# Binary cross-entropy on one core: the last chunk's predictions move in unequal pieces at both ends, and the side block goes

## The chip, the cores and the metric

The kernel runs on one core of one Trainium2 chip. The metric is device time in microseconds (us), the median of several runs; lower is better. Beside it stands one profiled execution, whose trace gives every instruction and every packet of the sixteen DMA engines. The engines named below are PE (TensorE, unused here), DVE (VectorE), ACT (ScalarE), POOL (GpSimd) and SP (SyncE). POOL and SP do no arithmetic here: they issue transfers, each from a queue of its own, in program order.

## The reference

```python
"pred": np.random.uniform(0.01, 0.99, (8192, 8192)).astype(np.float32),
"target": np.random.randint(0, 2, (8192, 8192)).astype(np.float32),
...
eps = 1e-7
pred = np.clip(pred, eps, 1 - eps)
return -(target * np.log(pred) + (1 - target) * np.log(1 - pred))
```

Each element stands alone, so the arrays can be cut in any way. Two arrays of 268 MB are read and one is written.

## The kernel before

A target is 0 or 1, so the loss is minus the logarithm of the absolute value of (target - 1 + pred). The kernel uses this: `front_of` (L89) clips the predictions on VectorE (L90), adds target minus 1 on VectorE (L93), takes the absolute value on ScalarE (L96) and the logarithm on ScalarE (L97). `back_of` (L99) changes the sign on VectorE (L100). All passes work in place on the predictions.

The flat arrays are taken from the end to the front in 37 chunks. Each is 128 partitions wide, with so many columns: two of 7680, then 32 of 15360, then two of 7680 and one of 1696. Spots in on-chip memory are given by `plan` (L15): two rings, one for predictions (float32) and one for targets (bfloat16, cast by the transfer on its way in), each with two places of 15360 columns used in turn, and a third small place for the last chunk alone. The last chunk is short by 352 columns, because the very first 45056 elements are a block of their own, the side block: 32 partitions of 1408, moved by SP in transfers of eight rows each, every fourth partition (L60 to L62, L78 to L87). It has two tiles of its own and goes through the same passes.

The order is written out by hand, and every engine follows it in program order. `load(k)` (L69) issues the targets of chunk k on POOL (L71) and the predictions on POOL (L72), for chunk 0 on SP. `store(k)` (L74) issues on POOL (L76), for the last three chunks on SP. In the main loop (L120) chunk k is worked in two halves and stored, and then chunk k+2 is loaded into the place that k leaves: its targets at once, its predictions after the whole store of k has landed. That wait is POOL's at L72, and what stands behind it on POOL is the next store.

The last four chunks are called z, a, b and c (L132). Chunk z has 15360 columns; a and b are the two halves, which share the place that chunk n-5 leaves; c is the small one. On VectorE the sign change of z's second half (L139) comes after both passes of chunk a (L138), and the store of z (L140) after that. Stores a, b and c are SP's. The target and prediction loads of a, b and c are all issued at the end of the last turn of the loop (L130 and L131).

A transfer runs on DMA engines in packets, one for each row of a partition: a chunk of 15360 columns is 128 packets of 61440 bytes for predictions, eight on each of the sixteen engines. Queue 0 in the trace is POOL's, queue 1 is SP's.

Of the kernel before, what the change touches and what calls it, by code (L numbers as in the profile page):

```python
# [1 line left out]

# [4 lines left out]

EPS = 1e-7

BIG = 15 * 1024  # L10
HALF = BIG // 2
SIDE = 1408


def plan(total):  # L15

    n, last = divmod(total, BIG)
    assert n > 4 and 0 < last <= 2048
    spots = [(HALF, 0), (HALF, HALF)]
    spots += [(BIG, k % 2 * BIG) for k in range(1, n - 1)]  # L20
    end = (n - 1) % 2 * BIG
    return spots + [(HALF, end), (HALF, end + HALF), (last - SIDE // 4, 2 * BIG)]

@with_exitstack
def kernel(
    ctx: ExitStack,
    tc: tile.TileContext,
    pred: bass.AP,  # L30
    target: bass.AP,
    out: bass.AP,
):
    nc = tc.nc
    fp32 = mybir.dt.float32
    bf16 = mybir.dt.bfloat16
    Alu = mybir.AluOpType
    Act = mybir.ActivationFunctionType
    P = nc.NUM_PARTITIONS

    R, C = pred.shape
    spots = plan(R * C // P)
    n = len(spots)
    widths = [w for w, _ in spots]
    cols = [sum(widths[:k]) for k in range(n)]

    def chunk(ap, k):
        flat = ap.rearrange("r c -> (r c)")
        end = R * C - cols[k] * P
        return flat[end - widths[k] * P : end].rearrange("(p w) -> p w", p=P)  # L50

    pool = ctx.enter_context(tc.tile_pool(name="rings", bufs=1))
    ring = [P, 2 * BIG + widths[-1]]
    ring_p = pool.tile(ring, fp32, name="ring_p", tag="ring_p")
    ring_t = pool.tile(ring, bf16, name="ring_t", tag="ring_t")
    warm = pool.tile([1, 8], fp32, name="warm", tag="warm")
    side_p = pool.tile([32, SIDE], fp32, name="side_p", tag="side_p")
    side_t = pool.tile([32, SIDE], fp32, name="side_t", tag="side_t")

    def side(ap, j):  # L60
        flat = ap.rearrange("r c -> (r c)")
        return flat[: 32 * SIDE].rearrange("(p w) -> p w", p=32)[j:32:4]  # L62

    def spot(ring, k, part=(0, 1)):
        w, c = spots[k]
        i, m = part
        return ring[:, c + i * w // m : c + (i + 1) * w // m]

    def load(k):  # L69
        queue = nc.sync if k == 0 else nc.gpsimd  # L70
        nc.gpsimd.dma_start(out=spot(ring_t, k), in_=chunk(target, k))  # L71
        queue.dma_start(out=spot(ring_p, k), in_=chunk(pred, k))  # L72

    def store(k):  # L74
        queue = nc.sync if k >= n - 3 else nc.gpsimd
        queue.dma_start(out=chunk(out, k), in_=spot(ring_p, k))  # L76

    def load_side():  # L78
        nc.vector.memset(side_p[:, 0:2], 0.5)  # L79
        nc.vector.memset(side_t[:, 0:2], 0.0)  # L80
        for j in range(4):
            nc.sync.dma_start(out=side_t[j:32:4, :], in_=side(target, j))
            nc.sync.dma_start(out=side_p[j:32:4, :], in_=side(pred, j))

    def store_side():
        for j in range(4):
            nc.sync.dma_start(out=side(out, j), in_=side_p[j:32:4, :])  # L87

    def front_of(p, t):  # L89
        nc.vector.tensor_scalar(  # L90
            out=p, in0=p, scalar1=EPS, scalar2=1 - EPS, op0=Alu.max, op1=Alu.min
        )
        nc.vector.scalar_tensor_tensor(  # L93
            out=p, in0=t, scalar=1.0, in1=p, op0=Alu.subtract, op1=Alu.add
        )
        nc.scalar.activation(out=p, in_=p, func=Act.Abs)  # L96
        nc.scalar.activation(out=p, in_=p, func=Act.Ln)  # L97

    def back_of(p):  # L99
        nc.vector.tensor_scalar(out=p, in0=p, scalar1=-1.0, scalar2=None, op0=Alu.mult)  # L100

    def front(k, *part):
        front_of(spot(ring_p, k, *part), spot(ring_t, k, *part))

    def back(k, *part):
        back_of(spot(ring_p, k, *part))

    with tc.manual_schedule():
        nc.vector.memset(warm, 1.0)  # L109
        for k in range(3):  # L110
            load(k)
        nc.scalar.activation(out=warm, in_=warm, func=Act.Ln)  # L112
        front(0)
        front(1)
        back(0)
        store(0)
        back(1)
        store(1)
        load(3)
        for k in range(2, n - 4):  # L120
            front(k, (0, 2))
            front(k, (1, 2))
            back(k, (0, 2))
            back(k, (1, 2))
            store(k)
            if k == n - 6:
                load_side()
            if k == n - 5:
                front_of(side_p, side_t)
            for j in range(k + 2, n if k == n - 5 else k + 3):  # L130
                load(j)  # L131
        z, a, b, c = range(n - 4, n)  # L132
        front(z, (0, 2))
        back_of(side_p)
        store_side()
        front(z, (1, 2))
        back(z, (0, 2))
        front(a)  # L138
        back(z, (1, 2))  # L139
        store(z)  # L140
        front(b, (0, 2))
        front(b, (1, 2))
        back(a)
        store(a)
        front(c)
        back(b)
        store(b)
        back(c)
        store(c)


# [1 line left out]
_INS = ['pred', 'target']  # L153
_OUTS = [((8192, 8192), 'float32')]


# [23 lines left out]
```

## Time and profile before

| What | Value | Where from |
|---|---|---|
| Time | 1864.74 us, median of 3 (1864.71, 1864.74, 1867.43) | times |
| Profiled execution: span | 1863.1 us | page |
| Profiled execution: its time | the span is all that is recorded of it; it lies 1.65 us below the median | page, times |
| Main memory read, written | 536.87 MB, 268.44 MB; 432 GB/s over the span | page, DMA queues |
| Store, issue to landing (15360 columns) | 29.2 us, median | page, DMA issues |
| Prediction load, issue to landing (15360) | 35.9 us, median | page, DMA issues |
| One transfer issue on POOL | 0.53 to 0.54 us | page, groups |
| Side block's passes | VectorE 0.87, 1.61 and 0.87 us; ScalarE 1.38 and 1.38 us | page, groups |

The page gives the busy share of each engine over the span, then the span in forty slices, then the DMA queues, the chain that ended last, and the costliest groups. The chain through the end of the kernel is read as start, length and what it was:

```profile
1749.26 4.17 DVE ring_p L100
1753.43 0.28 issue
1753.72 29.18 DMA out_dram<-ring_p
1782.89 0.28 issue
1783.18 18.44 DMA ring_p<-in_pred_dram
```

The store of chunk n-5 is issued at 1753.7 and has landed 29.18 us later; then the predictions of chunk a may be loaded into its place, and they land 18.44 us after that.

The side block's transfers stand in the list of issues with count, size and line:

```profile
side_t<-in_target_dram SPq DMA_DIRECT2D x4, 44.0 KB
side_p<-in_pred_dram SPq DMA_DIRECT2D x4, 44.0 KB
out_dram<-side_p SPq DMA_DIRECT2D x4, 44.0 KB
```

### The profile page before, as it was taken

The numbers are of one execution on the slowest core, as the hardware profiler recorded it, in microseconds if no ns is written. First come the engines' busy times: TensorE is split into PE (matmuls) and PEld (weight loads), VectorE is DVE, ScalarE is ACT, GpSimd is POOL, SyncE is SP. The second block draws the span as 40 slices with busy tenths as digits, with TensorE's granted clock in tenths as the row PEclk, the third lists the DMA queues.
The fourth block names the chain that finished last, engine by engine and source line by source line (L and its number), as shares of the span: only waits on it lengthen the run. The fifth ranks groups of instructions, "written<-read, shape, count | busy, mean of one in ns | idle before, by whom it ended". The sixth has DMA issues, their size and how long they took to land.

```text
span 1863.1 us, 649 instructions
## 1 busy us (share of the span) xinstructions
DVE 1124.7 (60%) x215; ACT 902.1 (48%) x144; POOL 57.4 (3%) x111
## 2 busy tenths in 40 slices
DVE  4655767555576655557665555766555576655585
ACT  3345553335555333555533355553335555333665
POOL 0000000000000000000000000000000000000000
DMA  9999999999999999999999999999999999999999
GB/s 295 378 356 343 352 344 367 383 385 348 348 352 344 370 384 383 347 352 351 346 370 385 383 347 352 351 346 370 385 383 346 352 352 346 370 384 379 352 340 392
DMA packets 16180, 671.22 MB, mean 360 GB/s; under 512 B 1872, under 2 KB 1872, under 8 KB 2352
## 3 DMA queue, kind: packets, MB, share of 16 engines
q0 software_dynamic: 15408, 657.98, 98.5%
q1 hardware_dynamic: 768, 13.21, 1.7%
q14 instruction: 4, 0.03, 0.0%
HBM read 536.87 MB, written 268.44 MB: 432 GB/s over the span
## 4 chain that ended last, share of the span: by engine, by line
DMA 35%; issue 26%; ACT 22%; DVE 15%; POOL 1%; DVEq 0%; POOLq 0%; PEldq 0%
DMA ring_p<-in_pred_dram 32%; ACT ring_p L96 11%; ACT ring_p L97 11%; DVE ring_p L93 7%; DVE ring_p L90 4%; DVE ring_p L100 4%; DMA out_dram<-ring_p 3%; POOL ring_t L71 0%; POOL out_dram L76 0%; DVEq L175 0%; POOL ring_p L72 0%; POOLq L76 0%; POOLq L71 0%; DVEq L90 0%; PEldq L175 0%
## 5 line engine op out<-in xcount | busy, mean ns | idle before, releaser
L96 ACT ACTIVATE ring_p<-ring_p 128x7680 f32<-128x7680 f32 (+1 forms) x70 | 450.3, 6433 | 932.2 <-DVE ring_p L93 932.2
L93 DVE SCALAR_TENSOR_TENSOR ring_p<-ring_t,ring_p 128x7680 f32<-128x7680 bf16 (+1 forms) x70 | 556.9, 7955 | 2.4
L90 DVE TENSOR_SCALAR ring_p<-ring_p 128x7680 f32<-128x7680 f32 (+1 forms) x70 | 283.8, 4055 | 396.7 <-DMA ring_p<-in_pred_dram 396.7
L100 DVE TENSOR_SCALAR ring_p<-ring_p 128x7680 f32<-128x7680 f32 (+1 forms) x69 | 283.8, 4115 | 321.2 <-ACT ring_p L97 321.2
L97 ACT ACTIVATE ring_p<-ring_p 128x7680 f32<-128x7680 f32 (+1 forms) x70 | 450.8, 6440 | 2.2
L72 POOL DMA_DIRECT2D ring_p<-in_pred_dram x36 | 19.2, 532 | 909.3 <-DMA out_dram<-ring_p 909.3
L76 POOL DMA_DIRECT2D out_dram<-ring_p x34 | 18.4, 541 | 851.3 <-DVE ring_p L100 827.0
L71 POOL DMA_DIRECT2D ring_t<-in_target_dram x37 | 20.0, 542 | 0.8 <-PEq L175 0.8
L96 ACT ACTIVATE side_p<-side_p 32x1408 f32<-32x1408 f32 x1 | 1.4, 1375 | 6.7 <-DVE side_p L93 6.7
L112 ACT ACT_TABLE_LOAD x1 | 1.3, 1283 | 0.7 <-PEq L164 0.7
L93 DVE SCALAR_TENSOR_TENSOR side_p<-side_t,side_p 32x1408 f32<-32x1408 f32 x1 | 1.6, 1611 | 0.0
L97 ACT ACTIVATE side_p<-side_p 32x1408 f32<-32x1408 f32 x1 | 1.4, 1375 | 0.0
L90 DVE TENSOR_SCALAR side_p<-side_p 32x1408 f32<-32x1408 f32 x1 | 0.9, 874 | 0.0
L100 DVE TENSOR_SCALAR side_p<-side_p 32x1408 f32<-32x1408 f32 x1 | 0.9, 874 | 0.0
L109 DVE MEMSET warm<- 1x8 f32 x1 | 0.1, 65 | 0.8 <-PEq L164 0.8
L112 ACT ACTIVATE warm<-warm 1x8 f32<-1x8 f32 x1 | 0.2, 209 | 0.0
L164 POOL MEMSET const-float32-0.0<- 128x1 f32 x1 | 0.1, 99 | 0.2 <-issue 0.2
L164 POOL MEMSET const-bfloat16-1.0<- 128x1 bf16 x1 | 0.1, 102 | 0.0
L164 POOL MEMSET const-float32-1.0<- 128x1 f32 x1 | 0.1, 99 | 0.0
L164 POOL MEMSET const-uint8-127<- 128x1 uint8 x1 | 0.1, 99 | 0.0
L79 DVE MEMSET side_p<- 32x2 f32 x1 | 0.1, 60 | 0.0
L80 DVE MEMSET side_t<- 32x2 f32 x1 | 0.1, 60 | 0.0
## 6 DMA issues: line engine op xcount, KB each, us to landing
ring_p<-in_pred_dram POOLq DMA_DIRECT2D x32, 7680.0 KB, 35.9
out_dram<-ring_p POOLq DMA_DIRECT2D x32, 7680.0 KB, 29.2
ring_t<-in_target_dram POOLq DMA_DIRECT2D x32, 3840.0 KB, 46.8
ring_p<-in_pred_dram POOLq DMA_DIRECT2D x3, 3840.0 KB, 35.6
ring_t<-in_target_dram POOLq DMA_DIRECT2D x4, 1920.0 KB, 27.9
out_dram<-ring_p POOLq DMA_DIRECT2D x2, 3840.0 KB, 27.1
out_dram<-ring_p SPq DMA_DIRECT2D x2, 3840.0 KB
ring_p<-in_pred_dram SPq DMA_DIRECT2D x1, 3840.0 KB
```

Source lines behind the costliest of these rows:

```text
L71: nc.gpsimd.dma_start(out=spot(ring_t, k), in_=chunk(target, k))
L72: queue.dma_start(out=spot(ring_p, k), in_=chunk(pred, k))
L76: queue.dma_start(out=chunk(out, k), in_=spot(ring_p, k))
L79: nc.vector.memset(side_p[:, 0:2], 0.5)
L80: nc.vector.memset(side_t[:, 0:2], 0.0)
L90: nc.vector.tensor_scalar(out=p, in0=p, scalar1=EPS, scalar2=1 - EPS, op0=Alu.max, op1=Alu.min)
L93: nc.vector.scalar_tensor_tensor(out=p, in0=t, scalar=1.0, in1=p, op0=Alu.subtract, op1=Alu.add)
L96: nc.scalar.activation(out=p, in_=p, func=Act.Abs)
L97: nc.scalar.activation(out=p, in_=p, func=Act.Ln)
L100: nc.vector.tensor_scalar(out=p, in0=p, scalar1=-1.0, scalar2=None, op0=Alu.mult)
L112: nc.scalar.activation(out=warm, in_=warm, func=Act.Ln)
L164: nc = _bacc.Bacc("TRN2", target_bir_lowering=False, num_devices=1)
```

## The change

The side block, its tiles, its transfers and its passes are gone. The last chunk has its full 2048 columns. Its rows are dealt out otherwise: the first 262144 elements are seen as (b a w) with b = 8, a = 16 and w = 2048, and partition 8a + b holds row 16b + a (`mixed`).

Its predictions come in pieces. A piece (j, lo, hi) covers the 32 partitions from 32j and the columns from 256 lo to 256 hi; in main memory its outer dimension is 4. Four pieces are issued after load 2, of widths 8, 6, 4 and 2 (in units of 256 columns) for j = 0, 1, 2, 3; three more after load 3, of widths 6, 4 and 2 for j = 3, 2, 1. Its targets are one transfer, issued where they were issued before. Its result is stored in eight pieces, on POOL instead of SP. All seven early pieces and the eight late ones are POOL's.

On POOL the early pieces stand ahead of the store of chunk 0, and ahead of the store of chunk 2. The eight late pieces stand behind the store of z, at the end of the queue. POOL's transfers take eight semaphores in turn, so the fourth early piece waits for the first target load, and the last late piece waits for the store of z.

```diff
-SIDE = 1408
+STEP = 256
+EARLY = ((0, 0, 8), (1, 0, 6), (2, 0, 4), (3, 0, 2), (3, 2, 8), (2, 4, 8), (1, 6, 8))
+LATE = (
+    (0, 0, 8), (1, 0, 1), (2, 0, 4), (3, 0, 6),
+    (1, 2, 8), (1, 1, 2), (3, 6, 8), (2, 4, 8),
+)
...
-    return spots + [(HALF, end), (HALF, end + HALF), (last - SIDE // 4, 2 * BIG)]
+    return spots + [(HALF, end), (HALF, end + HALF), (last, 2 * BIG)]
...
+    def mixed(ap):
+        flat = ap.rearrange("r c -> (r c)")[: widths[-1] * P]
+        return flat.rearrange("(b a w) -> a b w", b=8, a=16)
+
+    def tooth_of(ap, j, lo, hi):
+        return mixed(ap)[4 * j : 4 * j + 4, :, lo * STEP : hi * STEP]
+
+    def tooth_in(j, lo, hi):
+        return spot(ring_p, n - 1)[32 * j : 32 * j + 32, lo * STEP : hi * STEP]
+
+    def load_teeth(teeth):
+        for tooth in teeth:
+            nc.gpsimd.dma_start(out=tooth_in(*tooth), in_=tooth_of(pred, *tooth))
+
+    def store_teeth(teeth):
+        for tooth in teeth:
+            nc.gpsimd.dma_start(out=tooth_of(out, *tooth), in_=tooth_in(*tooth))
...
         for k in range(3):
             load(k)
+        load_teeth(EARLY[:4])
...
         load(3)
+        load_teeth(EARLY[4:])
...
-            if k == n - 6:
-                load_side()
-            if k == n - 5:
-                front_of(side_p, side_t)
-            for j in range(k + 2, n if k == n - 5 else k + 3):
+            for j in range(k + 2, n - 1 if k == n - 5 else k + 3):
                 load(j)
+        nc.gpsimd.dma_start(out=spot(ring_t, n - 1), in_=mixed(target))
         z, a, b, c = range(n - 4, n)
         front(z, (0, 2))
-        back_of(side_p)
-        store_side()
...
         back(c)
-        store(c)
+        store_teeth(LATE)
```

More of the change, by code (lines that the diff above doesn't have):

```diff
@@ L56 @@
     warm = pool.tile([1, 8], fp32, name="warm", tag="warm")
[L57 to L62, printed above, removed]
     def spot(ring, k, part=(0, 1)):
@@ L76, in store @@
         queue.dma_start(out=chunk(out, k), in_=spot(ring_p, k))
[L78 to L87, printed above, removed]
+    def mixed(ap):
[11 more added lines that the diff above has]
+            nc.gpsimd.dma_start(out=tooth_of(out, *tooth), in_=tooth_in(*tooth))
     def front_of(p, t):
```

## The prediction

> **What bounds the kernel now.** I read the busy shares first, then the table of windows, then the list of waits, then the timeline of the end, and last the records of single DMA packets.
>
> ```profile
> span 1863.1 us, 649 instructions
> DVE 1124.7 (60%) x215; ACT 902.1 (48%) x144; POOL 57.4 (3%) x111
> DMA  9999999999999999999999999999999999999999
> q0 software_dynamic: 15408, 657.98, 98.5%
> q1 hardware_dynamic: 768, 13.21, 1.7%
> ```
>
> No compute engine is busy above 60%, while the sixteen DMA engines are busy in every slice; the two queues add up to 100.2% of their time, since packets overlap a little. The windows say where that stops.
>
> ```profile
> 0.00:2.00 2.00, 0.07 (x1) 1.26 (x1) 0.96 (x6) 1.00 0.63 154
> ...
> 700.00:1700.00 1000.00, 602.48 (x113) 490.10 (x75) 29.41 (x56) 1.00 1.00 361
> ...
> 1820.00:1859.00 39.00, 24.41 (x9) 23.83 (x8) 0.00 (x0) 1.00 0.99 425
> 1859.00:1863.10 4.10, 0.00 (x0) 0.00 (x0) 0.00 (x0) 1.00 0.31 129
> ```
>
> The last-but-one column is the DMA share: 1.00 over the middle, 0.99 to 1859, then 0.31. Only the last 4 us leave engines idle. So the time is the work of the engine that ends last, plus its idle time, plus 2.0 us before the first packet and 1.05 us from the last packet (1862.05) to the end.
>
> ```profile
> POOL ring_p L72 <- DMA out_dram<-ring_p: 909.3, 32, 29.2
> DVE ring_p L90 <- DMA ring_p<-in_pred_dram: 396.7, 36, 18.5
> ```
>
> These waits are long, but the engines have queued packets under them. One stage has little cover, the end:
>
> ```profile
> 1801.71 4.16 DVE L90 TENSOR_SCALAR ring_p<-ring_p 128x7680 f32<-128x7680 f32 x1 [7.08 <-DMA ring_p<-in_pred_dram]
> 1805.91 8.16 DVE L93 SCALAR_TENSOR_TENSOR ring_p<-ring_t,ring_p 128x7680 f32<-128x7680 bf16 x1
> 1813.98 4.15 DVE L100 TENSOR_SCALAR ring_p<-ring_p 128x7680 f32<-128x7680 f32 x1
> 1818.43 0.54 POOL L76 DMA_DIRECT2D out_dram<-ring_p  x1 [32.62 <-DVE ring_p L100]
> ...
> 1836.52 9.95 SPq L76 DMA_DIRECT2D out_dram<-ring_p  x3
> ```
>
> VectorE works in order, so the store of z (L76 on POOL) waits for chunk a's predictions on all sixteen engines (1801.7), a's first two passes and z's sign change. Its first packets start at 1819.85, 1.42 us after the issue began; three engines had by then been empty for 0.2 us. Those three pay again at 1838.2, where store a arrives just as they finish z: their first packets take 1.81 to 1.98 us instead of 1.138.
>
> **Packet prices.** 61440 B take 2267 ns, 30720 B 1138, 6784 B 258: about 9 ns plus 0.03675 ns a byte. By that line, less 3 ns of overlap, eight rows cost 2.46 us at 8192 B, 1.85 at 6144, 1.25 at 4096, 0.65 at 2048 and 0.35 at 1024.
>
> **Collisions and drift.** At 73 us, where the third load ends and the first store begins, the sixteen last load packets take 2.48 to 3.23 us, together 9.6 us too much. The next such borders cost 3.0, 2.8, 0.4, 2.8, 0.9, 2.0, 1.2, 1.2, 1.2 and 1.4 us, then almost nothing. All come to 27 engine-us, 1.7 us a mean engine. Chained by start times, the engines lie 0.7 us apart at 26 us and 3.9 us apart from 856 us on (1.4 ahead of the mean to 2.5 behind). They end between 1859.2 and 1862.05, mean 1860.65.
>
> **The change part by part.**
>
> *Side block gone.* Its 96 packets of 5632 B (221 ns) fall away. The records show eight completion writes per side transfer, sixteen per whole one, so it used eight engines: 12 x 0.22 = 2.6 us on those, 1.35 us a mean engine. Its vector and scalar passes (3.4 and 2.8 us) lay in idle time: nothing.
>
> *Last chunk.* Its old load and store of predictions (8 x 0.255 = 2.04 us each) go; its target load grows from 2.03 to 2.45 us an engine (1696 to 2048 wide).
>
> *Pieces.* Early ones, if successive transfers take successive groups of four engines: group 0 gets widths 8 and 6 (2.46 + 1.85 = 4.31 us), group 1 3.10, group 2 1.90, group 3 0.65. Late ones go on with group 3: 4.31 there, then 0.70, 1.90 and 3.10 on groups 0, 1, 2. Each group has 5.0 us in all. Work per engine: minus 2.04, 2.04 and 1.35, plus 0.42, 5.0 and some 0.15 for completion writes: +0.1 us, level.
>
> [...] No transfer of before on POOL uses fewer than sixteen engines.
>
> *POOL's queue.* Fifteen issues of 0.54 us join. The fourth early piece waits for the first target load's semaphore; behind it stands the store of chunk 0, not ready before 56.6. The next three follow load 3 (95.6), ahead of a store due at 119.8. The last late piece waits for store z (landed by 1843); the late issues begin about 1846.3 and end about 1850.6, under stores a and b (running to 1857). SP loses thirteen issues; its two stores wait on VectorE as before. Cover holds: nothing. Without it each POOL issue would add its 0.54 us.
>
> *Collisions with groups apart.* Gain between 0 and 1.7 us a mean engine. With four engines together instead of sixteen I take half: 0.9 remains. A latest engine may keep between 0 and 4.2 (1.7 + 2.5).
>
> *The gate at the end.* The stagger must be paid where all engines wait for the slowest. Old loads b, target c and predictions c kept an engine busy for 22.2 us after a's predictions; without the last load it is 18.1 + 2.45 = 20.55. Store z arrives 18.15 us after the slowest landing. So an engine more than 2.4 us ahead runs dry. Group 3 is 3.66 us ahead of group 0: it idles 1.3 us or more and ends last.
>
> *Sum along group 3.* The three early engines of before go from 1819.85 to 1857.13 (z, a, b and both stalls); group 3 repeats that, then 4.31 of late pieces, 1.05 of closing: 1862.5, shifted by d, by which a's predictions land later. Before, the mean engine ended the last load at 1822.0 and the latest at 1823.7. Without side and collisions the mean is 1822.0 - 1.35 - 1.7 = 1818.95; group 0 has 4.31 more and 0.35 of initial spread: 1823.6, so d = -0.1 plus the collisions left, 0.9: 0.8. Span 1863.3, +0.2 us.
>
> *Speed of the pieces.* Group 0 and group 1 each write 32 neighbouring rows at once; no row shows that. Bounds: the line (side packets 221 ns where it gives 216), and the stretch that two engines at one place would give, twice. I take the line, the nearest in shape.
>
> The median of the three runs is 1.65 us above the profiled span, so the forecast is 1864.9 us.
>
> **Rivals.**
>
> *B, stagger at no cost.* No collisions, no gate: target c ends at 1818.95 - 2.04 + 0.42 = 1817.3 without pieces; + 5.0 of pieces + 36.3 (z, a, b) + 0.15 + 0.35 + 1.05 = 1860.1, median 1861.8 (-0.16%). For it: borders free of stretch after 700 us. Against: the 18.15 us of the gate.
>
> *D, slower: pieces at half speed.* Groups 0 and 1 write rows 0 to 31 and 32 to 63 at the same time; if pairs of engines share an entrance, group 0's early pieces take 4.31 us more and every later landing with them; if reading back also halves, group 3's late ones take 4.31 more. 1864.9 + 8.6 = 1873.5 (+0.47%). For it: stretches of up to 1.43 times at the borders. Against: side packets at full speed. It decides from about 0.43 us per 8192 B packet (0.31 by the line), where 2 x 4.31 x 0.41 = 3.5 us take the forecast past +0.2%.
>
> [...]
>
> *C, no rotation.* All pieces fall on one group: 1817.3 + 10.0 + 0.35 + 0.9 + 36.3 + 10.0 + 0.15 + 1.05 = 1876.05, median 1877.7 (+0.7%). For it: nothing seen; against: nothing seen.
>
> *E, the change does not stagger:* the pieces spread over sixteen engines, collisions stay. The latest engine: 1817.3 + 2.5 + 0.35 + 4.2 + 36.3 + 2.5 + 0.15 + 1.05 = 1864.35, median 1866.0. Against: eight engines for eight rows in the side block.
>
> **How the numbers follow.** Forecast 0.55 (own range 1862.5 to 1868), B 0.12, D 0.15, C 0.10, E 0.08. About 0.2% is what a measurement here can tell from no change, so the bounds are 1861.0 and 1868.5. Faster: 0.05, from B's lower half. Slower: C, most of D and the forecast's upper tail, 0.27. Same: 0.68. The range, 1861.5 to 1870, leaves out C, D's upper half (0.07) and B's edge (0.03).
>
> **What would show it.** Right: fifteen new transfers, engines in four groups 1.2 us apart after load 3; fewer stretched packets at 73 to 675 us; a's predictions used near 1802.5; a dip of DMA share near 1820; the last packets on group 3. Wrong: 8192 B packets well over 0.31 us (D); four engines ending 10 us after the rest (C); no groups (E); no dip and engines level (B). A run outside the range would mean a cost in the stores or loads of the main loop that I have at nothing.

## The result and the profile after

| | Before | After |
|---|---|---|
| Median of 8 runs each | 1865.35 us (1864.71 to 1867.43) | 1870.56 us (1869.84 to 1871.31) |
| Profiled execution, span | 1863.1 us | 1869.5 us (its time: 1871.31 us) |

After takes 1.0028 times the time of before, 95% interval 1.0018 to 1.0038: slower by 0.28%, or 5.2 us. The profiled execution of after is the slowest of its eight, 0.75 us above the median, so the 6.4 us between the two spans overstate the loss a little.

The page of after, its shares and the groups of the new lines (the times behind the bar are busy us, then mean ns of one, then the idle time before them):

```profile
span 1869.5 us, 634 instructions
DVE 1122.2 (60%) x210; ACT 900.2 (48%) x142; POOL 67.1 (4%) x125
DMA  9999999999999999999999999999999999999998
q0 software_dynamic: 17040, 659.31, 98.4%
q1 hardware_dynamic: 432, 11.80, 1.6%
...
L88 POOL DMA_DIRECT2D ring_p<-in_pred_dram x7 | 5.3, 760 | 16.4 <-DMA ring_t<-in_target_dram 16.4
L92 POOL DMA_DIRECT2D out_dram<-ring_p x8 | 4.7, 595 | 30.9 <-issue 30.9
```

The picture of the whole is the old one: no compute engine above 60%, transfers in every slice. Seven early and eight late issues are there. One thing differs, the last digit of the DMA line: 8 instead of 9. The windows open it. Columns: stretch, its length, VectorE, ScalarE, POOL, granted clock, DMA share, GB/s; a packet is counted where it starts, so a short window can show more than 1.

```profile
700.00:1700.00 1000.00, 602.71 (x111) 493.14 (x75) 28.90 (x54) 1.00 1.00 361
...
1819.00:1822.00 3.00, 2.27 (x1) 3.00 (x1) 0.43 (x1) 1.00 0.61 157
1841.00:1842.00 1.00, 1.00 (x2) 0.97 (x2) 0.00 (x0) 1.00 0.00 0
...
1863.00:1867.00 4.00, 0.00 (x0) 0.00 (x0) 0.00 (x0) 1.00 0.52 169
```

In before the first of the three late windows reads:

```profile
1819.00:1822.00 3.00, 2.16 (x1) 2.97 (x2) 0.00 (x0) 1.00 1.15 410
```

The middle has not changed. Three holes have come at the end. From 1819 to 1822 the engines start little (0.61 against 1.15), at 1841 no packet starts at all, and from 1863 to 1867 about half of the engines still work, when before has ended. The packet records name no engine, so I chained them: each packet goes to the engine whose last packet ended where it starts. The chains give the idle time, summed over the sixteen engines (engine-us): 23.5 from 1819 to 1823, 17.0 from 1841 to 1843, and 33.5 from each engine's last data packet to the latest engine's (23.3 in before). The timeline says what the first two waited for (start, length, engine, line):

```profile
1804.85 4.16 DVE L95 TENSOR_SCALAR ring_p<-ring_p 128x7680 f32<-128x7680 f32 x1 [6.51 <-DMA ring_p<-in_pred_dram]
1809.05 8.16 DVE L98 SCALAR_TENSOR_TENSOR ring_p<-ring_t,ring_p 128x7680 f32<-128x7680 bf16 x1
1817.12 4.15 DVE L105 TENSOR_SCALAR ring_p<-ring_p 128x7680 f32<-128x7680 f32 x1
...
1821.57 0.55 POOL L74 DMA_DIRECT2D out_dram<-ring_p  x1 [32.54 <-DVE ring_p L105]
...
1824.79 2.16 DVE L95 TENSOR_SCALAR ring_p<-ring_p 128x3840 f32<-128x3840 f32 x1 [3.51 <-DMA ring_p<-in_pred_dram]
...
1841.51 7.86 SPq L74 DMA_DIRECT2D out_dram<-ring_p  x2
```

It is the stage that the prediction named, only later. Chunk a's predictions are used at 1804.85 (before 1801.71: 3.1 us later), so the store of z is issued 3.1 us later (1821.57 against 1818.43). Chunk b's predictions then come 19.94 us after a's, where before needed 18.10:

```profile
1819.81 2.16 DVE L90 TENSOR_SCALAR ring_p<-ring_p 128x3840 f32<-128x3840 f32 x1 [1.67 <-DMA ring_p<-in_pred_dram]
```

Chunk b's two halves stand ahead of a's sign change on VectorE, so the store of a is issued 5.0 us later (1841.51 against 1836.52). Each time most engines have run dry, and twelve of the sixteen start the store of z together, between 1822.70 and 1822.84: most of the stagger that the early pieces built is gone there. The late pieces are unequal in order to undo it. With little left to undo, they leave engines unequal at the end; the last data packet ends at 1867.22.

The long waits, as before, lie under queued packets:

```profile
POOL ring_p L70 <- DMA out_dram<-ring_p: 918.0, 32, 33.8
...
DVE ring_p L95 <- DMA ring_p<-in_pred_dram: 404.1, 36, 18.8
...
POOL ring_p L88 <- DMA ring_t<-in_target_dram: 16.4, 1, 16.4
```

L88 is the fourth early piece, behind the first target load's semaphore for 16.4 us, as forecast; the store of chunk 0 was not ready, and no engine ran dry.

Last, the packet records of the pieces. The durations are means in us over one size; the first column is what the prediction's line gives. Rows under 4096 bytes appear merged into packets of 4096: the first four pieces have 32 rows of 4096 and 32 of 2048, and the records 48 packets of 4096.

```
bytes   line    early, 75-80 us   early, 132-137 us   late
8192    0.310   0.486             -                   0.381
6144    0.235   0.353             0.246               0.292
4096    0.160   0.285             0.180               0.201
```

The first four pieces are slow, up to 0.679 us for 8192 bytes, and the late ones partly.

### The profile page after: what moved, and what is told of

Read it like the earlier page. It is cut to its first block, busy times and chain, and to the rows that moved or that the text cites. A ratio compares the mean times of both kernels' runs of the same rounds, so it can differ in the third digit from the quotient of the medians.

```text
span 1869.5 us, 634 instructions
## 1 busy us (share of the span) xinstructions
DVE 1122.2 (60%) x210; ACT 900.2 (48%) x142; POOL 67.1 (4%) x125
## 4 chain that ended last, share of the span: by engine, by line
DMA 36%; issue 25%; ACT 22%; DVE 15%; POOL 1%; DVEq 0%; POOLq 0%; PEldq 0%
DMA ring_p<-in_pred_dram 33%; ACT ring_p L102 11%; ACT ring_p L101 11%; DVE ring_p L98 7%; DVE ring_p L105 4%; DVE ring_p L95 4%; DMA out_dram<-ring_p 3%; POOL ring_t L69 1%; POOL out_dram L74 0%; POOL out_dram L92 0%; DVEq L177 0%; POOL ring_p L70 0%; POOLq L177 0%; POOLq L74 0%; POOLq L70 0%
## 5 line engine op out<-in xcount | busy, mean ns | idle before, releaser
L70 POOL DMA_DIRECT2D ring_p<-in_pred_dram x35 | 18.7, 534 | 918.0 <-DMA out_dram<-ring_p 918.0
L74 POOL DMA_DIRECT2D out_dram<-ring_p x34 | 18.4, 540 | 824.1 <-DVE ring_p L105 824.1
L88 POOL DMA_DIRECT2D ring_p<-in_pred_dram x7 | 5.3, 760 | 16.4 <-DMA ring_t<-in_target_dram 16.4
L92 POOL DMA_DIRECT2D out_dram<-ring_p x8 | 4.7, 595 | 30.9 <-issue 30.9
```

The lines of the kernel that those rows point to most:

```text
L88: nc.gpsimd.dma_start(out=tooth_in(*tooth), in_=tooth_of(pred, *tooth))
L92: nc.gpsimd.dma_start(out=tooth_of(out, *tooth), in_=tooth_in(*tooth))
```

## The experiments

Each ratio is to the kernel before on the same chip, where its medians were 1865.85 to 1866.3 us. Engine-us are sums over the sixteen engines; sixteen of them are 1 us of a mean engine. In the expectations, the gate theory puts the loss on engines that run dry before the late stores, the layout theory on the rows that each engine writes.

### The parts alone: no side block, an early load

e1_no_side is before without the side block, its last chunk 2048 wide, in ordinary order.

> The kernel before without its side block; the last chunk has its full 2048 columns and stays on all sixteen engines, loaded and stored where it was. Layout theory (the loss comes from rows that engines write or read through a common entrance) and gate theory (the loss comes from engines held apart at stores z and a) both expect about the kernel before, 1864.5 to 1867: the work per engine is level, but the 2.6 us that the side block put on eight engines no longer balance the drift, so the last engine may end up to 1.3 us later. Above 1868 would mean that the side block itself was worth what the change lost.

Measured: 1866.11 us, ratio 1.0000 (0.9991 to 1.0010). The side block costs nothing that a measurement with this interval, about 0.1%, can tell, and so gives nothing back.

e2_early_whole adds the early load, as one whole transfer, without pieces or dealing:

```diff
             load(k)
+        nc.gpsimd.dma_start(out=spot(ring_p, n - 1), in_=chunk(pred, n - 1))
...
-            for j in range(k + 2, n if k == n - 5 else k + 3):
+            for j in range(k + 2, n - 1 if k == n - 5 else k + 3):
                 load(j)
+        nc.gpsimd.dma_start(out=spot(ring_t, n - 1), in_=chunk(target, n - 1))
```

> As e1, and the last chunk's predictions are loaded in one transfer on sixteen engines after load 2. Gate theory: removing 2.4 us of queue ahead of store z lets every engine more than 2.4 us ahead of the slowest run dry near 1820; with the drift of before (3.9 us) that is up to 1.5 us on a few engines, so e1 plus 0 to 1.5 us. Layout theory: e1 to within 0.5 us.

Measured: 1865.56 us, ratio 0.9997 (0.9988 to 1.0007). Loading c early is free too, to the same interval. Most of its 8192-byte packets are at the line (median 0.309 us), but not all: their mean is 0.379 and the longest takes 0.665, in ordinary row order. The engines idle only 4.6 engine-us from 1700 to 1832. So most of what is slow in after comes with the pieces, their rows or their order, and a part of its slow early packets belongs to the place, between a load and a store.

### Unequal pieces, or the way the rows are dealt

e3_equal_pieces is after with four equal pieces, all after load 2, and four equal late ones: no stagger is built or undone.

```diff
-EARLY = ((0, 0, 8), (1, 0, 6), (2, 0, 4), (3, 0, 2), (3, 2, 8), (2, 4, 8), (1, 6, 8))
-LATE = (
-    (0, 0, 8), (1, 0, 1), (2, 0, 4), (3, 0, 6),
-    (1, 2, 8), (1, 1, 2), (3, 6, 8), (2, 4, 8),
-)
+EARLY = ((0, 0, 8), (1, 0, 8), (2, 0, 8), (3, 0, 8))
+LATE = EARLY
...
         load(3)
-        load_teeth(EARLY[4:])
```

> The changed kernel with equal pieces: four early ones of full width, one for each group, and four late ones, so that nothing is staggered; rows and four engines each as in the changed kernel. Gate theory: the stagger is gone, so the loss goes: 1864 to 1867, stretched packets at the store borders come back. Layout theory: the pieces and the last target load still meet at common entrances, each 8192 B packet well over 0.31 us early, and the last packets of chunk b's predictions stretched by 0.3 to 0.5 us: 1868 to 1871.

Measured: 1870.64 us, ratio 1.0023 (1.0014 to 1.0032). The loss is all there without unequal widths, so the reading that put it on the stagger alone falls. The early packets are slower still: 0.557 us in the mean, up to 0.784.

e4_own_rows was to give each engine ordinary rows: eight pieces of 16 neighbouring rows, all after load 2.

```diff
+ROWS = (0, 16, 64, 80, 32, 48, 96, 112)
...
     def tooth_of(ap, j, lo, hi):
-        return mixed(ap)[4 * j : 4 * j + 4, :, lo * STEP : hi * STEP]
+        rows = chunk(ap, n - 1)[ROWS[j] : ROWS[j] + 16, lo * STEP : hi * STEP]
+        return rows.rearrange("(a b) w -> a b w", a=4)
```

> As e3, but in eight pieces of 16 rows, ordered so that each group of four engines handles the rows that it handles in a whole transfer, and the last target load in the usual row order. Layout theory: 2 us or more under e3, 8192 B packets at 0.31 us, no stretch of chunk b's packets: 1864 to 1867. Gate theory: as e3.

Measured: 1880.29 us, ratio 1.0075 (1.0060 to 1.0090), a miss for both theories, since it was not the kernel that I meant. With neighbouring rows in main memory the pieces did not stay on four engines: the sixteen packets of the last one start together, between 81.61 and 81.79 us. So sixteen engines wrote sixteen neighbouring rows at a time, at 0.592 us in the mean over all eight pieces. And eight pieces in a row behind five loads filled POOL's eight semaphores: at their line (L83 there) the wait list has five waits, as many as the loads, and a second kind of wait among them, for load 2 itself:

```profile
POOL ring_p L83 <- DMA ring_t<-in_target_dram: 37.8, 3, 16.4
...
POOL ring_p L83 <- DMA ring_p<-in_pred_dram: 26.9, 2, 18.2
```

The store of chunk 0 stood behind it, and the engines ran dry for 2.5 us:

```profile
79.50:82.00 2.50, 2.47 (x2) 0.00 (x0) 2.50 (x3) 1.00 0.21 59
```

Two costs at once, so its time settles nothing; that neighbouring rows are slow on sixteen engines too is its one use.

e5_dealt_whole changes the row order of the last chunk and nothing else: e1, with c dealt as in after, but in whole transfers on sixteen engines.

```diff
+        if k == n - 1:
+            return flat[: widths[k] * P].rearrange("(b a w) -> a b w", b=8, a=16)
```

> e1 with one thing changed: the last chunk's rows are dealt out as in the changed kernel (partition 8a + b holds row 16b + a), but its predictions, its targets and its result go in whole transfers on sixteen engines, where they went before. Layout theory (engines meet at common entrances because each handles eight neighbouring rows): 8192 B packets of the load at about 0.6 us instead of 0.31, chunk b's last packets stretched, stores z and a late: 2 to 5 us over e1, 1868 to 1871. Rival, that transfers on four engines are the cost: e1 to within 0.5 us, packets at 0.31.

Measured: 1868.43 us, ratio 1.0013 (1.0003 to 1.0022), 2.3 us over e1. The row order costs without any piece. Its packets of c's predictions take 0.447 us (0.311 in e1), and the loads beside them suffer: chunk b's packets together take 8.9 engine-us too long (0.2 in e1), single ones up to 1.20 us. That moves the moment at which b's predictions are used by almost 3 us. e1, then e5:

```profile
1801.66 4.16 DVE L72 TENSOR_SCALAR ring_p<-ring_p 128x7680 f32<-128x7680 f32 x1 [6.50 <-DMA ring_p<-in_pred_dram]
...
1819.75 2.16 DVE L72 TENSOR_SCALAR ring_p<-ring_p 128x3840 f32<-128x3840 f32 x1 [1.67 <-DMA ring_p<-in_pred_dram]
```

```profile
1801.83 4.16 DVE L74 TENSOR_SCALAR ring_p<-ring_p 128x7680 f32<-128x7680 f32 x1 [6.47 <-DMA ring_p<-in_pred_dram]
...
1822.61 2.16 DVE L74 TENSOR_SCALAR ring_p<-ring_p 128x3840 f32<-128x3840 f32 x1 [4.36 <-DMA ring_p<-in_pred_dram]
```

Chunk a's predictions come at the same time in both (1801.7, 1801.8); b's at 1819.75 and 1822.61. No engine runs dry for it (1.3 engine-us idle in e5, 1.2 in e1): the 2.3 us lie in the packets alone. Which rows an engine gets is an estimate of mine from the transfer's outer dimension, here and below; the records don't name them. And the order in main memory changes together with the order on chip, so e5 prices the two as one.

e6_own_rows_four is the kernel that e4 should have been: equal pieces of 16 rows on four engines, each engine with four neighbouring rows, where dealing main memory in steps of 32 rows was to hold them; four pieces after load 2, four after load 3.

```diff
-        return flat.rearrange("(b a w) -> a b w", b=8, a=16)
+        return flat.rearrange("(b q w) -> q b w", b=4, q=32)
...
-        return mixed(ap)[4 * j : 4 * j + 4, :, lo * STEP : hi * STEP]
+        q = ROWS[j] // 4
+        return dealt(ap)[q : q + 4, :, lo * STEP : hi * STEP]
...
-        load_teeth(EARLY)
+        load_teeth(EARLY[:4])
...
         load(3)
+        load_teeth(EARLY[4:])
```

> As e3 with equal pieces on four engines each, but pieces of 16 rows in which each engine has four neighbouring rows and no two engines of the sixteen share a block of 4 + 4 rows 32 apart; four pieces after load 2, four after load 3, eight at the end. The last target load is dealt by fours and stays as crossed as in e3. Layout theory: early and late 8192 B packets back to 0.31 to 0.40 us, and 1.5 to 3 us under e3: 1867.5 to 1869; chunk b's packets still stretched. Rival, that four engines each or short pieces are the cost: e3 or slower, 1870 to 1872, packets at 0.5 or more.

Measured: 1867.45 us, ratio 1.0007 (0.9997 to 1.0016), 3.2 us under e3. I had expected chunk b's packets still to be stretched, since the rows were dealt; they weren't (0.2 engine-us, as in e1). So it is not dealing as such: eight neighbouring rows per engine are slow (0.557 us in e3, 0.447 in e5), four are not, although rows of main memory are dealt out in both, in steps of 16 and of 32. The pieces run at 0.357 and 0.332 us early, no slower than e2's whole transfer, and at 0.309 late. Chunk b's predictions come 18.1 us after a's again; in e3 it was 20.15:

```profile
1805.16 4.16 DVE L92 TENSOR_SCALAR ring_p<-ring_p 128x7680 f32<-128x7680 f32 x1 [6.43 <-DMA ring_p<-in_pred_dram]
...
1825.31 2.16 DVE L92 TENSOR_SCALAR ring_p<-ring_p 128x3840 f32<-128x3840 f32 x1 [3.73 <-DMA ring_p<-in_pred_dram]
```

```profile
1804.72 4.16 DVE L94 TENSOR_SCALAR ring_p<-ring_p 128x7680 f32<-128x7680 f32 x1 [6.51 <-DMA ring_p<-in_pred_dram]
...
1822.82 2.16 DVE L94 TENSOR_SCALAR ring_p<-ring_p 128x3840 f32<-128x3840 f32 x1 [1.67 <-DMA ring_p<-in_pred_dram]
```

But a's are as late in e6 as in e3 (1804.72), and engines idle 14.9 engine-us ahead of the store of z. e6 differs from e3 in the number of pieces as well, so the clean price of the row order is e5's, 2.3 us.

### The gate at the end

If the late stores of z and a cost time by themselves, an order on VectorE that frees them sooner must give it back. e7_after_early_z takes z's last sign change between a's halves; e8_early_whole_early_z does the same to e2.

```diff
-        front(a)
+        front(a, (0, 2))
         back(z, (1, 2))
         store(z)
+        front(a, (1, 2))
         front(b, (0, 2))
-        front(b, (1, 2))
         back(a)
         store(a)
+        front(b, (1, 2))
         front(c)
```

> The changed kernel with another order at the end on VectorE: chunk a's front in two halves with z's last sign change between them, and a's sign change ahead of b's second half, so that stores z and a are issued about 6 us earlier. Gate theory: the empty time before stores z (near 1820) and a (near 1842) goes; both cost 1.1 to 1.4 us of mean engine, so 1867.5 to 1869.5. Layout theory alone: the engines' own work is unchanged and sets the end, 1870 to 1871.

> e2 with the order at the end of e7. Gate theory: the few engines that ran dry in e2 no longer do, 0 to 1.5 us under e2: 1864 to 1865.5. Otherwise e2 to within 0.5 us.

Measured: e7 1872.68 us, ratio 1.0033 (1.0020 to 1.0046); e8 1866.48 us, ratio 1.0002 (0.9993 to 1.0011). Both missed. The engines had work at 1819 and at 1841, but the wait had moved: b's second half now comes after a's sign change, so the store of b is late, and the engines stand still before it (e7):

```profile
1848.00:1853.00 5.00, 4.60 (x2) 4.08 (x3) 0.00 (x0) 1.00 0.24 104
```

That is 66.3 engine-us idle from 1847 to 1854 in e7, and 44.9 before store b in e8. An order can't be judged by the gate that it opens alone. e11_after_split_tail is after with an order that opens all three, and b's store in halves; e12_early_split_tail is e2 with it.

```diff
-        front(a)
+        front(a, (0, 2))
         back(z, (1, 2))
         store(z)
+        front(a, (1, 2))
+        back(a, (0, 2))
         front(b, (0, 2))
-        front(b, (1, 2))
-        back(a)
+        back(a, (1, 2))
         store(a)
+        front(b, (1, 2))
+        back(b, (0, 2))
+        store_half(b, 0)
         front(c)
-        back(b)
-        store(b)
+        back(b, (1, 2))
+        store_half(b, 1)
```

> The changed kernel with the end rearranged without putting chunk b off: a's front and its sign change in halves around z's and b's work, and store b in two halves. Gate theory: the empty time near 1820 and 1842 goes (22 and 17 engine-us, 2.4 us of mean engine) and none comes at store b: 1868 to 1869.5, against 1870.5. If it stays within 0.5 us of the changed kernel, the empty time at the end cost it nothing by itself.

> e2 with the end of e11. Few engines ran dry in e2 (some 6 engine-us), so e2 minus 0 to 0.7 us: 1864.8 to 1865.6.

Measured: e11 1867.94 us, ratio 1.0010 (1.0001 to 1.0019), 2.6 us under after (3.1 us when each is set against before on its own chip); e12 1866.39 us, ratio 1.0002 (0.9993 to 1.0011), 0.8 us over e2, a miss. The windows of e11 at the places where after had its holes:

```profile
1819.00:1822.00 3.00, 3.00 (x2) 0.96 (x1) 0.00 (x0) 1.00 1.36 474
1841.00:1842.00 1.00, 0.96 (x2) 0.97 (x2) 0.00 (x0) 1.00 0.64 276
1863.00:1867.00 4.00, 0.00 (x0) 0.00 (x0) 0.00 (x0) 1.00 0.02 4
```

Between packets no engine idles before z, a or b, and the last microseconds are almost empty. The row order is still slow in e11 (early 8192-byte packets 0.468 us in the mean), and it stays 2.1 us over before; what that rest is made of is taken up below.

e12 shows why opening the gate need not pay. The gaps are gone there (1.3 engine-us over the whole run, 6.7 in e2), but from each engine's last data packet to the latest one's it idles 50.3 engine-us, where e2 idles 13.1. One reading is that the gate had held the early engines back to the slow ones, and that without it their lead is idle time at the end; no run tests this reading.

### Does a stagger do anything

With own rows (four neighbouring ones per engine, as in e6) and the widths levelled out before the end, the stagger can be tried by itself. e9_own_rows_level is e6 with early widths 7, 5, 3, 1, the rest loaded in the last turns of the loop so that every engine has the same sum, and one whole store of c on SP; e10_own_rows_even is the same with widths of 4.

```diff
-EARLY = tuple((j, 0, 8) for j in range(8))
-LATE = EARLY
+WIDE = (7, 5, 3, 1)
+EARLY = tuple((j, 0, WIDE[j % 4]) for j in range(8))
+REST = tuple((j, WIDE[j % 4], 8) for j in range(8))
...
+            if k in (n - 7, n - 6):
+                load_teeth(REST[4 * (k - n + 7) : 4 * (k - n + 7) + 4])
...
-        store_teeth(LATE)
+        nc.sync.dma_start(out=dealt(out), in_=spot(ring_p, n - 1))
```

> The own rows of e6, staggered and levelled again before the end: early pieces of widths 7, 5, 3, 1 (four after load 2, four after load 3), the rest of each row (1, 3, 5, 7) after two of the last loads of the main loop, the result in one whole store. If staggering does take the collisions at the store borders away (27 engine-us, 1.7 us of mean engine in the kernel before), and nothing else is lost, it is 1 to 2.5 us under e10 and may come under the kernel before: 1863 to 1865.5. If the engines' drift does not cost the end anything, equal to e10.

> As e9 with widths 4 everywhere: the same number of pieces, rows and places, no stagger. Stretched packets at the borders as in the kernel before. 1865.5 to 1867.

Measured: e9 1865.35 us, ratio 0.9996 (0.9987 to 1.0004); e10 1866.93 us, ratio 1.0004 (0.9995 to 1.0013). The stagger is worth the 1.6 us between them: e9's borders cost 25.6 engine-us of stretched packets up to 700 us and its engines idle 1.4 ahead of the store of z, against 32.5 and 9.3. It pays back no more than the pieces seem to cost (e10 lies 1.1 us over before, within its interval). Beside before, e9 can't be told from no change, and no kernel here beats before.

## Why the prediction was wrong

The time, 1870.56 us, lies 5.7 us above the forecast and just above the range, on the slower side, which had 0.27. The steps that failed are the speed of the pieces, taken from the line, the new row order, taken as free, and the size of the gate. The two rivals about the grouping fall: the engines stand in four groups (at 204 us four of them start within 0.28 us, the others 1.3 to 1.6, 2.4 to 2.9, 3.4 and 4.2 to 4.8 us later), so neither "no rotation" nor "the change does not stagger" holds, nor "stagger at no cost". That successive pieces take successive groups, an if in the prediction's sums, the chains of after show behind load 3: between 131.5 and 136.4 us four engines carry no piece, four carry four packets of 4096 bytes each (the piece of width 2, merged), four eight of 4096 and four eight of 6144. By the prediction's own steps:

- *Side block, last chunk, POOL's queue:* costed at nothing on the path, and e1 and e2 agree (ratios 1.0000 and 0.9997). The wait of the fourth piece is there (16.4 us) and covered.
- *Collisions:* I took half of 1.7 us as the gain. From 73 to 700 us the stretched packets at the borders come to 6.2 engine-us against 29.4 in before (27 by the narrower count of the prediction): 1.45 us of a mean engine, more than forecast. The borders at 71 and 131 us keep 1.5 and 1.7 engine-us, the later ones next to nothing.
- *Speed of the pieces* is the step that failed first: "I take the line, the nearest in shape". The 8192-byte packets took 0.486 us early and 0.381 late. That is past the 0.43 from which D decides, but not D's double, and only partly late. D's cause, that engines meet where groups 0 and 1 write rows 0 to 31 and 32 to 63, no run shows: e5 has slow packets (0.447) with no group at all, e6 has groups with 0.357 and less. Some of the early stretch is not row order either, since e2 has 0.379 at the same place.
- *The target load's new row order* was costed by its length alone, 2.45 us. The rows that an engine gets were taken for free. It stretches chunk b's prediction packets beside it: 8.7 engine-us too long in after, single packets by up to 0.57 us (0.2 engine-us in before). e5 shows this cost without pieces, and e5 - e1 = 2.3 us prices the row order as a whole.
- *d* was mis-sized: 0.8 forecast, 3.1 measured. The early packets take 16.8 engine-us more than the line gives, 1.0 us of a mean engine, and the spread of the engines is 4.84 us from 150 us on (3.66 forecast for the groups), 6.2 by 1617 us.
- *The gate at the end* was the right mechanism at the right place, with the wrong size and one store too few: 1.3 us or more on group 3 were forecast; 23.5 engine-us before z, about 1.5 us of a mean engine, and another 17.0, about 1.1 us, before the store of a, which I had not counted. That second one comes from b's late predictions.
- *Sum along group 3:* z's first packets 2.3 us later than the forecast (d); from there to the last packet 44.5 us instead of 41.6, by store a's wait and the slow late pieces, whose stretch does not fall on one group; closing 0.95 us longer than forecast. Together 6.2 us, from the forecast span of 1863.3 to 1869.5.
- *Readings:* the prediction's packet times lie 0.24 us late against the timeline's zero. On that zero the first packet starts at 1.75 us, the last ends at 1861.81, the closing is 1.27 us, and the store of z starts 1.17 us after its issue began. Sums along packets are untouched; the 18.15 us of the gate, taken between a packet and the timeline, are 17.9.
- *Work of a mean engine:* forecast level, less the collisions; the records have 2.0 us more. The pieces take 6.6 us instead of 5.0, the completion writes 0.46 more instead of 0.15, chunk b's packets 0.5 and those of stores a and b 0.8, against 1.4 saved at the borders.

What is the loss made of? The chained records divide each profiled span into the packets of a mean engine, the gaps between them, the wait of the engines that end early for the latest one, and the closing after the last data packet (the start, 1.9 to 2.0 us, is left out). In us:

```
              before   after    e1       e5       e11
packets       1858.3   1860.3   1858.8   1861.0   1859.3
gaps             0.1      2.9      0.1      0.1      0.3
uneven end       1.5      2.1      2.1      2.3      2.2
closing          1.3      2.2      1.2      1.2      2.2
```

The spans of before and after lie 6.4 us apart: packets 2.0, gaps 2.8, the uneven end 0.6, the closing 1.0. The row order shows in e5 against e1, 2.2 us of longer packets and next to nothing else. The slow packets of after (pieces and chunk b, 35 engine-us over the line) come to as much, before what the borders save. The gate shows in e11 against after: 2.6 us of gaps, and 1.0 us of packets, since the packets of stores a and b, stretched by 15.4 engine-us in after, are at their length there. The two are not independent: the slow rows make a part of the lateness at the gate. What e11 keeps over before, 2.9 us in the spans, is packets 1.0, the uneven end 0.8 and the closing 1.0; that it is near e5's amount is chance. The closing is 1.6 us or more in every kernel that ends with POOL's pieces (6.1 in e4) and 1.2 to 1.3 where SP stores c whole; the prediction had it the same for both, and its cause stays open.

With good rows, the gate and the pieces without stagger together cost 1.15 us over before (e6), not separable from nothing. Not tried: own rows with after's stagger and e11's order together, and a row order changed on chip alone.

What makes the rows slow is not shown. In sign the runs agree: with eight neighbouring rows an engine's packets take 0.557 us in e3 and 0.447 in e5, with four 0.357 and 0.332 early, where e2's whole transfer has 0.379, and 0.309 late (e6). In e4, where sixteen engines write sixteen neighbouring rows at a time, the packets of the last piece take 0.41 to 0.45. That the order of rows decides is shown, by the 2.3 us of e5 over e1; where the packets meet is not, and a part played by the order in main memory is not excluded.

## What to carry to other kernels

Where the DMA engines are always busy, as here (a share of 1.00 from 700 to 1700 us), the rows that each engine moves can be part of a transfer's price (2.3 us in e5): change the row order alone, in one whole transfer, before building on it, and look at the neighbours' packets too. A stagger that still stands where every engine must wait for the slowest is paid there as idle time, in after 23.5 engine-us before the store of z; find that place (here VectorE's order around chunk a's landing) and its cover, and count every store behind it. An order that opens one gate can close the next (e7: 66.3 engine-us before the store of b), or move the idle time to the end (e12: 50.3), so divide the whole span before and after, not one window.

## What the runs showed that I had not expected

- A piece on four engines writes on the idle ones as well: each piece of 32 rows brought 112 writes of 4 bytes, recorded singly or merged to 8 and 16 bytes, mostly at 9 ns a record. In the chains, engines that carried no piece have such writes too: from 131.47 to 131.62 us one has 24 such records between two packets of 61440 bytes. Fifteen pieces make 15 x 112 = 1680 more, and 3376 in all on POOL's queue; a transfer on all sixteen engines brought 16.
- With neighbouring rows in main memory a split did not hold: in e4 a pattern of 4 by 4 rows ran on sixteen engines, not four (the sixteen packets of its last piece start within 0.18 us).
- Instruction fetches are packets too (four of 8192 bytes in after, 0.03 MB on a queue of their own). They stand at 467, 621, 632 and 1446 us and take 0.309 us each. From 150 to 1617 us the spread of the engines grew from 4.84 to 6.2 us, by these and by packets stretched beside them.
- POOL issued the first late piece at 1853.02, 2.9 us after VectorE's last pass had ended (1850.15). The profile gives no cause, "issue" alone; stores a and b were still running under it.

```profile
1853.02 4.70 POOL L92 DMA_DIRECT2D out_dram<-ring_p  x8 [30.90 <-issue]
```
